# Spacing the small-matmul steps of a planned transformer kernel, with first column tiles interleaved

## The chip, the cores and the metric

The kernel runs on one core of a Trainium2 chip. Times are device microseconds from start to end of one execution. The kernel before takes 2018.91 us, the median of three runs (2014.14 to 2020.16).

## The reference, cut to what matters

A sequence of 256 positions with 1024 features goes through two blocks of two layers, all in fp32. A layer of the first block is a gated feed-forward (2816 wide), an attention mixer, and a second gated feed-forward. A layer of the second is a mixer of three branches and a feed-forward with a short convolution.

```python
def first_block(x, ...):
    for l in range(2):
        x = x + 0.5 * swiglu(rms_norm(x, norm_ffn1[l]), ...)
        x = x + hybrid_mixer(rms_norm(x, norm_mix[l]), ...)   # NSA heads (8) and MoBA heads (8), then w_out
        x = x + 0.5 * swiglu(rms_norm(x, norm_ffn2[l]), ...)
    return rms_norm(x, norm_final)

def second_block(x, ...):
    for l in range(2):
        p = rmsnorm(x, norm1_g[l]) @ w_in[l]
        p_rw, p_ret, p_sg, gate_logits = jnp.split(p, in_cuts, axis=-1)
        branches = jnp.stack([rwkv7_branch(p_rw, ...), retention_branch(p_ret, ...), sgu_branch(p_sg, ...)], axis=2)
        proj = jnp.einsum('bsgc,gcd->bsgd', branches, w_branch[l])
        x = x + jnp.sum(sigmoid(gate_logits) * proj, axis=2) @ w_out[l]
        x = x + conv_ffn(rmsnorm(x, norm2_g[l]), ...)
    return rmsnorm(x, final_g)

# the end of rwkv7_branch: a recurrence over the positions, then a norm by head
    y = rwkv7_scan(r, decay, k, v, kk, a)
    mean = jnp.mean(y, axis=-1, keepdims=True)
    var = jnp.mean(jnp.square(y - mean), axis=-1, keepdims=True)
    y = (y - mean) * lax.rsqrt(var + RW_GN_EPS) * lnx_g + lnx_b
    y = y + jnp.sum(r * k * r_k, axis=-1, keepdims=True) * v     # the "bonus"
    return y * g
```

NSA attention adds three gated parts for each head: attention over compressed keys, over selected keys and over a window. MoBA is attention over blocks of keys. Both are softmax attention with masks.

## The kernel before, in words

Every large product is done in three matmuls. ACT rounds a weight tile of 128x1024 (`raw`) to a high part `wh`, DVE subtracts it to get the low part `wl`, and the activations have a high and a low part too (`xx`, `yTh` and `yTl`, `oTh`, `h` and `hl`). The products are wh by high, wl by high and wh by low. In the profile they are the tiles `pj` (projections), `cf` (up projections of the feed-forwards) and `acc` (products back to 1024 features). They are the main stream, written out in the order of the layers. All weights come from device memory once, by transfers that SP issues.

Everything else is a side task: a Python generator that issues a few instructions, and yields until something is ready. A planner (`Builder`, with a clock for each engine in `Meter`) orders the instructions while the program is built; on the chip each engine then runs its instructions in that fixed order and waits for semaphores. After each group of main matmuls the main stream calls `tick`, which issues weight transfers, and then runs the steps of side tasks that are ready by the planner's clock, those of the lowest rank first. Where the main stream needs a side task's result, it calls `need`. That runs side steps one after the other until the result is planned, and no main matmul comes between.

The attention mixer (`mixer1`) projects queries, keys, values and gates, and runs the attention as side steps under the later projections and under the output product (`acc` from `oT`). `compressed` is the branch over compressed keys: scores `sc`, a softmax on DVE and ACT (`cs`, `cm`, `ce`), transposes, `pv`. `attend` handles the other parts: scores `sc`, a minimum on DVE (`sm`, `mn`), exponentials on ACT (`pe`), a product on DVE with `rsum`, transposes into PSUM (`pt`), a copy by ACT (`pts`), and the product with the values (`pv`).

The mixer of the second block (`mixer2`) first projects the RWKV columns (`mixed`, seven column tiles of 256, each in two halves of the depth). Side tasks then make the keys, queries and products of the recurrence. `rw_queries` lets POOL make r*k, whose sum by head is a small matmul `pb` (the bonus). `rw_chain` solves the recurrence in chunks: matmuls `pS` take `sa` and `X` in turns, and give `X` (DVE) and `sa` (ACT). At its end, for each 128 positions, `pY` is added to `Y`, and `group_norm` runs on it: a mean `gm` (DVE), squares `gsq` (ACT), their sum `gs` (DVE), `var` and `rstd` (POOL), four products or sums with `Y` (DVE), and POOL's `gbv`, which is the bonus times v plus lnx_b. `Y` is then transposed (`pt`) and split into `yTh` and `yTl`. `retention` does the like for `yret` (small matmuls `rs` and `py`) and `gating` for the spatial gate (`pm`, `su`, `sv`).

The main stream of `mixer2` goes on with the projections of retention and gating, and then, for each branch b in the order 1 (retention), 2 (gating), 0 (RWKV), with two halves of gates and two halves of the branch's projection (`proj`, PSUM ring "ps"), whose result DVE multiplies into `gate`. A branch's projection calls `need` for its `yTh`.

`load_wc` brings the five tiles of the weights that compress keys and values (`wc`), 2.6 MB, ahead of an attention mixer. It is called when the phase before that mixer begins, which in the first layer is at the start of the program.

Of the kernel before, what the change touches and what calls it, by code (L numbers as in the profile page):

```python
# [27 lines left out]
BIG = 3.0e38  # L28
# [173 lines left out]
class Task:  # L202
# [3 lines left out]
    def __init__(self, gen, rank):  # L206
        self.gen, self.rank = gen, rank
        self.ready = 0.0
        self.cond = None


ROWS = {"w0": 0, "lnx_g": 512, "lnx_b": 1024, "ln_g": 1536, "ln_b": 2048}
RWC = {"mu": (0, 14), "a0": (14, 4), "k_k": (18, 4), "k_a": (22, 4), "r_k": (26, 4)}
RET, SG, GATE = 1792, 3328, 4352
RW_GROUPS = (("wag", 1536, 256), ("k", 512, 512), ("r", 0, 512), ("v", 1024, 512))
# [2 lines left out]
LEAD = 1  # L218
FIRST = 2
PARTS, SKEW = 2, 2  # L220


class Builder:
    def __init__(self, tc, ctx, A, out):
        self.tc, self.A, self.out = tc, A, out
        self.meter = Meter()
        nc = self.nc = Engines(tc.nc, self.meter)
        self.cp = ctx.enter_context(tc.tile_pool(name="cp", bufs=1))
        self.wp = ctx.enter_context(tc.tile_pool(name="wp", bufs=NRAW))
        self.up = ctx.enter_context(tc.tile_pool(name="up", bufs=5))  # L230
        self.sp = ctx.enter_context(tc.tile_pool(name="sp", bufs=1))
        self.pp = ctx.enter_context(tc.tile_pool(name="pp", bufs=8, space=bass.MemoryType.PSUM))
        self.dp = ctx.enter_context(tc.tile_pool(name="dp", bufs=2, space=bass.MemoryType.DRAM))
        self.tasks = []
        self.plan, self.dma_next, self.high_next, self.split_next, self.take_next = [], 0, 0, 0, 0
        self.freed = self.lagged = 0
        self.raws, self.highs, self.parts = {}, {}, {}
        self.halves = [2, 2]
# [31 lines left out]
        self.tasks.sort(key=lambda x: x.rank)  # L270

    def step(self, task):
        self.meter.last = self.meter.t["PE"]
        try:
            y = next(task.gen)
        except StopIteration:
            self.tasks.remove(task)
            return
        if y is None:
            task.ready = self.meter.last + 0.1  # L280
        elif isinstance(y, float):
            task.ready = self.meter.last + y
        elif callable(y):
            task.cond = y
        else:
            task.ready = self.meter.of(y) + 0.1
# [10 lines left out]
    def tick(self, limit=3.0):  # L297
        m = self.meter
        end = m.t["PE"] + limit
        between = any(x.rank < 0 for x in self.tasks)  # L300
        if not between:
            self.fetch(self.lagged)
        while m.t["PE"] < end:
            late = m.t["DVE"] > m.t["PE"] + 5.0
            task = next((x for x in self.runnable() if x.ready <= m.t["PE"] and not (late and x.rank > 2)), None)
            if task is None:
                break
            self.step(task)
        if between:
            self.fetch(self.lagged, PACE)  # L310
        self.lagged = self.freed
# [877 lines left out]
    def mixer2_plan(self, l):  # L1189
        w_in, w_b = self.A["w_in_2"][l], self.A["w_branch_2"][l]  # L1190

        def cols(c0, n=512):
            self.proj_plan(w_in, 0, KD, c0, n)

        def branch(b):
            for hf in range(2):
                self.proj_plan(w_b[b], 0, 4, hf * 512, 512)

        for _, c0, n in RW_GROUPS:
            for c in range(c0, c0 + n, 2 * P):  # L1200
                for k0 in (0, 4):
                    self.plan.append((self.rows_of(w_in, k0 * P, 4, c, 2 * P), 4, 2 * P))
        for c0 in (RET, RET + 512, RET + 1024, SG + 512, SG):
            cols(c0)
        for b in (1, 2, 0):
            cols(GATE + b * D)
            cols(GATE + b * D + 512)
            branch(b)
        self.accum_plan(self.A["w_out_2"][l], 0, KD)

    def mixed(self, l, st, name, c0, n):


        nc = self.nc
        factor, factored = self.factor, self.factored
        done = st.setdefault("mixed", [])
        m = []

        def mix(i, ps):
            f0 = c0 // P + 2 * i  # L1220
            yield lambda: len(factored) == NT
            yield factor
            R = factor[0][:, None, :S].to_broadcast([P, 2, S])
            u, o = self.u("up"), self.pairs(name)
            uv, ov = (x.rearrange(v, e=2) for x, v in ((u, "p (e s) -> p e s"), (o.rearrange("p e t f -> p (e t f)"), "p (e s) -> p e s")))
            nc.vector.tensor_tensor(uv, ps.rearrange("p (e s) -> p e s", e=2), R, ALU.mult)
            done.append(name)
            yield
            for e in range(2):
                nc.scalar.activation(ov[:, e], uv[:, e], AF.Copy, scale=st["omu"][:, f0 + e:f0 + e + 1])  # L1230
            yield
            for e in range(2):
                nc.vector.scalar_tensor_tensor(ov[:, e, 1:], uv[:, e, :-1], st["mu"][:, f0 + e:f0 + e + 1], ov[:, e, 1:],
                                               ALU.mult, ALU.add)
            m.append(o)
            yield
            if len(m) == n // (2 * P):
                st[name] = m

        for i in range(n // (2 * P)):  # L1240
            at = st["banks"] = st.get("banks", -1) + 1
            self.need(lambda: len(done) > at - (3 if at == 6 else 4))
            ps = self.ps("pj", "pq" if at == 6 else ("ps", "pq")[at % 2])
            for k0 in (0, 4):
                self.need(lambda: min(self.ready_xT) > k0 // 4)
                wh, wl = self.take(4, 2 * P)
                xs = [[x[:, k0 + k].rearrange("p t f -> p (t f)") for x in (self.xh, self.xl)] for k in range(4)]
                for f in range(2):
                    c = slice(f * S, (f + 1) * S)
                    w = slice(f * P, (f + 1) * P)  # L1250
                    for k in range(4):
                        for j, (a, b) in enumerate(((wh, xs[k][0]), (wh, xs[k][1]), (wl, xs[k][0]))):
                            nc.tensor.matmul(ps[:, c], a[:, k, w], b, start=k0 + k + f + j == 0,
                                             stop=k0 + k == KD - 1 and j == 2, skip_group_check=True)
                        if k == 3 and f == 1:
                            self.free()
                        self.tick()
            self.begin(mix(i, ps), 0)

    def mixer2(self, l, after):  # L1260
# [6 lines left out]
        st = {}  # L1267
# [24 lines left out]
        def branch(b, hf):  # L1292
            def get(kk, t):
                self.need(lambda: (b, t) in yT)
                h, lo = yT[b, t]
                return h[:, kk], lo[:, kk]

            def evac(t, ps):
                g = gates[b, hf][t]
                nc.vector.tensor_tensor(g, ps, g, ALU.mult)  # L1300
                if (hf, t) in G:
                    nc.gpsimd.tensor_tensor(G[hf, t], G[hf, t], g, ALU.add)
                else:
                    G[hf, t] = g

            self.proj(get, 4, 512, evac)

        GT = {}

# [306 lines left out]
    def rw_queries(self, l, st):  # L1616
# [9 lines left out]
        for q in range(2):  # L1626
            nc.gpsimd.tensor_tensor(r[q], r[q], k[q], ALU.mult)
        yield r
        pb = self.ps("pb")
        for t in range(NT):  # L1630
            for j in range(4):
# [49 lines left out]
    def rw_chain(self, l, st, done):  # L1681
# [57 lines left out]
            return sa  # L1739

        S0 = None
        for t in range(NT):
            if t:
                pX = self.ps("pX")
# [28 lines left out]
                    mm(pY2[:, j * P:(j + 1) * P], kr[j // 2][:, j % 2, t, 1], S0[:, j], start=True, stop=True)  # L1773
                tt(Y[t], pY2, Y[t], ALU.add)
            yield
            self.begin(self.group_norm(lnx, Y[t], v[t], st["bonus"][t], st["g"][t], lambda y, t=t: done(t, y)), 3)

    def group_norm(self, lnx, y, v, bonus, g, done):
        nc = self.nc
        tt = nc.vector.tensor_tensor  # L1780
        heads, wide = self.heads, self.wide
# [2 lines left out]
        nc.vector.tensor_scalar(m, m, 1.0 / 64, None, ALU.mult)  # L1784
        tt(heads(y), heads(y), wide(m), ALU.subtract)
        yield
        sq, bv = self.u("gsq"), self.u("gbv")
        nc.scalar.activation(sq, y, AF.Square)
        nc.gpsimd.tensor_tensor(heads(bv), heads(v), wide(bonus), ALU.mult)
        nc.gpsimd.tensor_tensor(bv, bv, lnx[1], ALU.add)  # L1790
        yield [sq]
        s2 = self.small("gs", 8)
        nc.vector.tensor_reduce(s2, heads(sq), AX.X, ALU.add)
# [21 lines left out]
def emit(tc, A, out, upto=None):  # L1815
    with ExitStack() as ctx:
# [39 lines left out]
        def enter(i, t):  # L1856
            if t == 0 and any(ph[0] != "norm" for ph in phases[i:]):
                b.new_xT()
            b.begin(before(i, t), -1 - i)

        gain(0)
        b.fetch(-NSPLIT, most=FIRST)
        b.load_x(1)
# [3 lines left out]
        for i, (kind, l, gi, w) in enumerate(phases):  # L1867
            gain(i + 1)
            if i + 1 < len(phases) and phases[i + 1][0] == "mix1" or kind == "mix1" and i == 0:
                b.wc = []  # L1870
                b.load_wc(phases[i + 1][1] if kind != "mix1" else l, 0, 5)
            b.rows_next = i + 1 == len(phases) or (phases[i + 1][0] == "norm" and True)
            after = lambda t: enter(i + 1, t)
            if kind == "ffn":
# [24 lines left out]
```

## Time and profile before

| what | value |
| --- | --- |
| median of three runs | 2018.91 us |
| profiled execution | 2018.39 us, span 2016.6 us, mean clock 0.994 |
| TensorE (PE) busy | 1973.9 us, 98% |
| DVE busy | 1395.5 us, 69% |
| ACT busy | 1084.6 us, 54% |
| POOL busy | 153.2 us, 8% |
| DMA | 343.85 MB, mean 171 GB/s |

All compute instructions have the line of one helper (L191), so a group is known by its tiles, as `pt<-ident,Y`: output, then inputs. PE is TensorE's matmuls, PEld its weight loads. In a row of the timeline the first column is the start, the second the duration of the group, x the number of instructions in it; in brackets stand the idle time of that engine ahead of it and what ended it. In a row of the windows, each engine has its busy time and its instructions, then come the granted clock of TensorE (1.00 is 2.4 GHz, 0.50 is 1.2 GHz), the share of DMA and its rate. The layers follow each other: the attention mixers lie at 199 to 338 us and 709.5 to 849 us, the mixers of the second block at 1034.5 to 1329.5 us and 1528.5 to 1814 us. The rest is feed-forward.

### The profile page before, as it was taken

The numbers are of one execution on the slowest core, as the hardware profiler recorded it, in microseconds if no ns is written. First come the engines' busy times: TensorE is split into PE (matmuls) and PEld (weight loads), VectorE is DVE, ScalarE is ACT, GpSimd is POOL, SyncE is SP. The second block draws the span as 40 slices with busy tenths as digits, with TensorE's granted clock in tenths as the row PEclk, the third lists the DMA queues.
The fourth block names the chain that finished last, engine by engine and source line by source line (L and its number), as shares of the span: only waits on it lengthen the run. The fifth ranks groups of instructions, "written<-read, shape, count | busy, mean of one in ns | idle before, by whom it ended". The sixth has DMA issues, their size and how long they took to land. (4 is left out here: it accounts for less than half of the span.)

```text
span 2016.6 us, 31964 instructions
## 1 busy us (share of the span) xinstructions
PE 1973.9 (98%) x12396; PEld 1694.9 (84%) x12396; DVE 1395.5 (69%) x2201; ACT 1084.6 (54%) x1753; POOL 153.2 (8%) x176
## 2 busy tenths in 40 slices
PE   8999999999999999999999999999999999999998
PEld 6898877898889887788888767899988777889997
DVE  5764676765666467577567957579956796668983
ACT  5653666654555367565447443456646544446652
POOL 0000100000000010000021031210001004110000
PEclk9999999999999999999999999999999899999999
DMA  8664733666765563366664344556565443565663
GB/s 283 221 191 153 216 95 115 190 197 186 228 196 177 182 199 104 99 207 180 195 192 137 108 139 134 185 175 188 182 195 169 128 147 111 171 192 182 186 190 95
DMA packets 246726, 343.85 MB, mean 171 GB/s; under 512 B 22064, under 2 KB 182192, under 8 KB 246448
## 3 DMA queue, kind: packets, MB, share of 16 engines
q1 hardware_dynamic: 244224, 340.20, 54.7%
q8 instruction: 97, 1.59, 0.3%
q10 hardware_dynamic: 2352, 1.63, 0.3%
q14 instruction: 53, 0.43, 0.1%
HBM read 339.68 MB, written 2.10 MB: 169 GB/s over the span
## 5 line engine op out<-in xcount | busy, mean ns | idle before, releaser
L191 DVE TENSOR_TENSOR wl<-raw,wh 128x1024 fp32r<-128x1024 f32 (+1 forms) x614 | 750.8, 1235 | 262.8 <-ACT wh L191 262.0
L191 ACT CAST wh<-raw 128x1024 fp32r<-128x1024 f32 (+1 forms) x614 | 638.0, 1047 | 531.8 <-PE cf L191 176.8
L191 PE MATMUL cf<-xx,wh 128*128 128x256 f32 (+1 forms) x3072 | 544.0, 325 | 4.7 <-ACT wh L191 4.0
L191 PEld LDWEIGHTS cf<-xx,wh 128*128 128x128 f32 x3072 | 446.5, 191 | 43.0 <-ACT wh L191 4.8
L191 PE MATMUL pj<-wh,xx 128*128 128x512 f32 (+1 forms) x1088 | 364.9, 398 | 2.4 <-ACT rg L191 0.9
L191 PE MATMUL cf<-xx,wl 128*128 128x256 f32 x2112 | 295.7, 283 | 1.3 <-DVE wl L191 1.3
L191 PEld LDWEIGHTS cf<-xx,wl 128*128 128x128 f32 x2112 | 280.7, 191 | 12.8 <-DVE wl L191 1.7
L191 PEld LDWEIGHTS pj<-wh,xx 128*128 128x128 f32 x1088 | 204.3, 189 | 54.0 <-issue 8.4
L191 PE MATMUL pj<-wl,xx 128*128 128x512 f32 (+1 forms) x544 | 210.7, 387 | 0.0
L191 PE MATMUL acc<-wh,h 128*128 128x512 f32 x528 | 207.0, 392 | 0.0
L191 PE MATMUL acc<-wh,hl 128*128 128x512 f32 x528 | 205.6, 389 | 0.0
L191 PE MATMUL acc<-wl,h 128*128 128x512 f32 x528 | 205.5, 389 | 0.0
L191 PEld LDWEIGHTS pj<-wl,xx 128*128 128x128 f32 x544 | 103.0, 189 | 17.1 <-DVE wl L191 1.0
L191 PEld LDWEIGHTS acc<-wh,hl 128*128 128x128 f32 x528 | 99.1, 188 | 20.9
L191 PEld LDWEIGHTS acc<-wl,h 128*128 128x128 f32 x528 | 99.2, 188 | 19.9
L191 PEld LDWEIGHTS acc<-wh,h 128*128 128x128 f32 x528 | 99.2, 188 | 19.9
L191 POOL TENSOR_SCALAR xv<-ss 128x1 f32<-128x1 f32 x24 | 15.8, 660 | 1120.7 <-ACT junk L191 1120.6
L191 DVE TENSOR_TENSOR up<-cf,up 128x256 f32<-128x256 f32 x144 | 54.1, 418 | 67.1 <-ACT up L191 67.1
L191 PE MATMUL pj<-xx,wh 128*128 128x256 f32 x448 | 85.5, 290 | 3.4 <-DVE xx L191 2.0
L191 ACT CAST xx<-xg 128x512 fp32r<-128x512 f32 x40 | 24.9, 621 | 105.0 <-DVE xg L191 104.7
L191 DVE SCALAR_TENSOR_TENSOR cs<-up,conv,cs 128x255 f32<-128x255 f32 (+1 forms) x176 | 77.2, 480 | 0.4
L191 PEld LDWEIGHTS pj<-xx,wh 128*128 128x128 f32 x448 | 70.0, 191 | 8.5 <-issue 3.3
(314 smaller groups left out, 2231.3 us busy)
## 6 DMA issues: line engine op xcount, KB each, us to landing
raw<-w_in SPq DMA_DIRECT2D x156, 512.0 KB, 4.3
raw<-w_ffn_gate SPq DMA_DIRECT2D x88, 512.0 KB, 4.6
raw<-w_ffn_up SPq DMA_DIRECT2D x88, 512.0 KB, 4.8
raw<-w_ffn_down SPq DMA_DIRECT2D x88, 512.0 KB, 4.3
raw<-ffn_w_up SPq DMA_DIRECT2D x88, 512.0 KB, 4.5
raw<-ffn_w_down SPq DMA_DIRECT2D x44, 512.0 KB, 4.3
raw<-w_out SPq DMA_DIRECT2D x32, 512.0 KB, 3.7
raw<-w_branch SPq DMA_DIRECT2D x24, 512.0 KB, 3.9
```

The lines of the kernel that those rows point to most:

```text
L191: return f(*args, **kw)
```

## The change

1. `APART`: the planner notes for each place in a side task's code whether the step from there used TensorE (`kinds`), and when the last such step ended on the planner's clock (`burst`). In `tick`, a task of rank 0 or more, whose next step is known to use TensorE, is not run within 4 us after the last such step. `need` has no such rule.
2. `mixed`: the first halves of the first two column tiles come one after the other, then their second halves. The plan of the weight tiles follows.
3. `rw_queries` yields for 1.2 us on the planner's clock between POOL's r*k and the `pb` matmuls.
4. `gbv` moves out of `group_norm` into `offsets`, which is called for both halves of the positions when the last part of `rw_chain` begins.
5. The second half of the projection of the last branch uses the PSUM ring "pq" in place of "ps".
6. Where a feed-forward stands before an attention mixer, `load_wc` is called tile by tile by a side task (`later`), after 16, 20, 24, 28 and 32 weight tiles of that phase.

```diff
+APART = 4.0
 def step(self, task):
+        at, t0 = task.at(), m.t["PE"]
...
+        if m.t["PE"] > t0:
+            self.burst = m.t["PE"]
+            self.kinds[at] = True
+        else:
+            self.kinds.setdefault(at, False)
 def tick(self, limit=3.0):
+        apart = m.t["PE"] < self.burst + APART
...
-            task = next((x for x in self.runnable() if x.ready <= m.t["PE"] and not (late and x.rank > 2)), None)
+            task = next((x for x in self.runnable() if x.ready <= m.t["PE"] and not (late and x.rank > 2)
+                         and not (apart and x.rank >= 0 and self.kinds.get(x.at(), False))), None)
 def mixed(self, l, st, name, c0, n):
+        for i in range(n // (2 * P)):
+            early = st.pop("early", None)
+            if early is not None:
+                ps = early
+            else:
+                ps = bank()
+                products(ps, 0)
+            if st["banks"] == 0:
+                st["early"] = bank()
+                products(st["early"], 0)
+            products(ps, 4)
 def mixer2(self, l, after):
-            self.proj(get, 4, 512, evac)
+            self.proj(get, 4, 512, evac, "pq" if b == 0 and hf else "ps")
 def rw_queries(self, l, st):
         yield r
+        yield 1.2
         pb = self.ps("pb")
 def rw_chain(self, l, st, done):
+        bvs = [self.offsets(lnx, v[t], st["bonus"][t]) for t in range(NT)]
...
-            self.begin(self.group_norm(lnx, Y[t], v[t], st["bonus"][t], st["g"][t], lambda y, t=t: done(t, y)), 3)
+            self.begin(self.group_norm(lnx, Y[t], bvs[t], st["g"][t], lambda y, t=t: done(t, y)), 3)
 def emit(tc, A, out, upto=None):
+        def later(l, base):
+            for n in range(5):
+                yield lambda: b.take_next >= base + 16 + 4 * n
+                b.load_wc(l, n, n + 1)
...
-                b.load_wc(phases[i + 1][1] if kind != "mix1" else l, 0, 5)
+                if kind == "mix1":
+                    b.load_wc(l, 0, 5)
+                else:
+                    b.begin(later(phases[i + 1][1], b.take_next), 0)
```

The order of TensorE's instructions in the first attention mixer, in the NSA part (`sc` scores, `pt` transposes of `pe`, `pv` products with values, `pj` projections of the main stream). Before:

```order
L191 MATMUL pt<-ident,pe 128x128 x4
L191 MATMUL pj_2613<-wh,xx 128x512
L191 MATMUL pj_2613<-wl,xx 128x512
L191 MATMUL pj_2613<-wh,xx 128x512
L191 MATMUL pj_2614<-wh,xx 128x512
L191 MATMUL pj_2614<-wl,xx 128x512
L191 MATMUL pj_2614<-wh,xx 128x512 x2
L191 MATMUL pj_2614<-wl,xx 128x512
L191 MATMUL pj_2614<-wh,xx 128x512
L191 MATMUL pv<-pts,kv_1942 64x128 x2
L191 MATMUL pv<-pts,kv_2122 64x128 x2
```

The same place in the changed kernel, TensorE again:

```order
L191 MATMUL pt<-ident,pe 128x128 x4
L191 MATMUL pv<-pts,kv_1942 64x128 x2
L191 MATMUL pv<-pts,kv_2097 64x128 x2
L191 MATMUL sc<-kh,qst 128x512
L191 MATMUL sc<-kl,qst 128x512
L191 MATMUL sc<-kh,qst 128x512
L191 MATMUL sc<-kl,qst 128x512
L191 MATMUL pt<-ident,pe 128x128 x4
```

Nine projection matmuls stood between the transposes and the `pv` that needs ACT's copy of them; now none does. In the first layer no projection matmul comes after the transposes of `ce`, in the second only three come after the last transposes of the queries.

TensorE's order at the end of the recurrence of the second layer of the second block. Before (`pj_16788` is a gate's projection; the transposes of this `Y` come 60 main matmuls after the last `pY`):

```order
L191 MATMUL pY<-sa,mrb 64x64 x16
L191 MATMUL pY_16950<-S_16648,kr 128x128 x4
L191 MATMUL pj_16788<-wh,xx 128x512
L191 MATMUL pj_16788<-wl,xx 128x512
L191 MATMUL pj_16788<-wh,xx 128x512 x2
```

The same place after (`pj_17421` and `pj_17422` are the projection of the last branch, which needs `yTh`):

```order
L191 MATMUL pj_17421<-wh,yTl 128x512
L191 MATMUL pS<-sa,Lo 32x64 x4
L191 MATMUL pS<-X,dbd 32x64 x4
L191 MATMUL pY<-sa,mrb 64x64 x16
L191 MATMUL pY_17465<-S_16968,kr 128x128 x4
L191 MATMUL pt<-ident,Y 128x128 x4
L191 MATMUL pj_17422<-wh,yTh 128x512
```

The end of the recurrence moved into the last branch. Its transposes now follow the last `pY` at once; in the first layer three main matmuls stand between. The `pS` steps ahead of it stand 21 main matmuls apart.

TensorE's order in the second layer where the first branch (`pj_16636`, `pj_16637`) asks for the result of retention, `yret`, after:

```order
L191 MATMUL pj_16636<-wh,yTl 128x512
L191 MATMUL pX<-vt,lm 64x64 x2
L191 MATMUL pY<-vt,lm 64x64 x2
L191 MATMUL pX<-vt,lm 64x64 x2
L191 MATMUL pY<-vt,lm 64x64 x2
L191 MATMUL py<-rv,rsc 128x128
...
L191 MATMUL pt<-ident,yret 128x128 x4
L191 MATMUL pt<-ident,su 128x128 x4
L191 MATMUL pj_16637<-wh,yTh 128x512
```

Here side steps alone stand between two main matmuls; before, this branch found all of `yret` planned.

## Rows read from the trace of the kernel before

**Rows 1.** The page's head.

```profile
span 2016.6 us, 31964 instructions
PE 1973.9 (98%) x12396; PEld 1694.9 (84%) x12396; DVE 1395.5 (69%) x2201; ACT 1084.6 (54%) x1753; POOL 153.2 (8%) x176
```

**Rows 2.** Windows of the four mixers: busy time by engine, then clock and DMA.

```profile
199.00:338.00 139.00, 135.47 (x867) 107.41 (x866) 94.88 (x273) 90.74 (x213) 7.16 (x11) 1.00 0.43 133
709.50:849.00 139.50, 135.97 (x871) 107.93 (x870) 95.11 (x275) 91.28 (x214) 8.02 (x12) 1.00 0.44 136
1034.50:1329.50 295.00, 282.63 (x1860) 229.63 (x1858) 210.30 (x318) 149.99 (x235) 56.68 (x55) 0.98 0.48 150
1528.50:1814.00 285.50, 279.37 (x1838) 226.91 (x1836) 206.61 (x311) 145.33 (x228) 48.09 (x43) 0.98 0.50 155
```

**Rows 3.** Windows of an attention tail and of the stretches at half clock.

```profile
286.00:302.00 16.00, 13.86 (x119) 10.34 (x116) 10.53 (x26) 10.35 (x28) 0.00 (x0) 1.00 0.15 45
1103.84:1110.64 6.80, 6.71 (x26) 5.98 (x26) 5.22 (x15) 3.66 (x6) 0.04 (x1) 0.50 0.65 232
1240.40:1243.70 3.30, 3.30 (x9) 2.55 (x8) 2.05 (x3) 0.58 (x1) 0.00 (x0) 0.50 0.80 253
1592.00:1602.10 10.10, 10.10 (x42) 8.22 (x41) 4.92 (x14) 2.91 (x5) 1.36 (x1) 0.50 0.37 123
```

**Rows 4.** TensorE's waits: us in total, times, longest.

```profile
PE pj L191 <- DVE gate L191: 3.3, 2, 2.8
PE pb L191 <- POOL r L191: 2.0, 2, 1.4
PE pt L191 <- DVE v L191: 1.6, 1, 1.6
```

**Rows 5.** Timeline of the start, TensorE.

```profile
27.30 2.14 PE L191 MATMUL cf<-xx,wh 128*128 128x512 f32 x8 [1.31 <-ACT wh L191]
33.52 0.74 PE L191 MATMUL cf<-xx,wl 128*128 128x256 f32 x4 [1.30 <-DVE wl L191]
```

**Rows 6.** Timeline of a main run between small matmuls: its first, and the next small.

```profile
1111.69 0.50 PE L191 MATMUL pj<-wh,xx 128*128 128x512 f32 x1
1113.96 0.34 PE L191 MATMUL pX<-vt,lm 128*64 128x64 f32 x4
```

**Rows 7.** Timeline of the first NSA attention, TensorE.

```profile
282.64 0.66 PE L191 MATMUL pv<-pts,kv 128*64 128x128 f32 x8
284.62 0.47 PE L191 MATMUL pj<-wh,xx 128*128 128x512 f32 x1
288.83 1.57 PE L191 MATMUL pv<-pts,kv 128*64 128x128 f32 x16 [0.68 <-ACT pts L191]
291.76 0.43 PE L191 MATMUL pv<-pts,kv 128*64 128x128 f32 x2 [0.34 <-ACT pts L191]
```

**Rows 8.** Timeline of the compressed branch's softmax, first and last step, DVE.

```profile
255.33 0.29 DVE L191 SCALAR_TENSOR_TENSOR cs<-sc,cst 128x128 f32<-128x128 f32 x1 [0.36 <-PE sc L191]
260.75 0.29 DVE L191 TENSOR_TENSOR ce<-ce,cm 128x128 f32<-128x128 f32 x1
```

**Rows 9.** Timeline of the end of the first recurrence: DVE, TensorE, ACT.

```profile
1226.64 0.69 DVE L191 TENSOR_TENSOR Y<-pY,Y 128x512 f32<-128x512 f32 x1 [0.39 <-PE pY L191]
1234.29 0.69 DVE L191 TENSOR_TENSOR Y<-Y,rstd 128x512 f32<-128x512 f32 x1 [1.84 <-POOL rstd L191]
1238.21 1.28 DVE L191 TENSOR_TENSOR gate<-pj,gate 128x512 f32<-128x512 f32 x2
1238.95 0.50 PE L191 MATMUL pj<-wh,yTh 128*128 128x512 f32 x1 [2.80 <-DVE gate L191]
1240.39 0.59 ACT L191 CAST yTh<-pt 128x512 fp32r<-128x512 f32 x1 [3.11 <-PE pt L191]
```

**Rows 10.** Timeline of the end of retention, TensorE.

```profile
1182.12 0.48 PE L191 MATMUL py<-R,qs 64*128 64x128 f32 x2
1186.08 0.60 PE L191 MATMUL pt<-ident,yret 128*128 128x128 f32 x4
```

More of the change, by code (lines that the diff above doesn't have):

```diff
@@ L209, in __init__, with at @@
         self.cond = None
+    def at(self):
+        r, g = [], self.gen
+        while g is not None and getattr(g, "gi_frame", None) is not None:
+            r.append((g.gi_code.co_name, g.gi_frame.f_lineno))
+            g = g.gi_yieldfrom
+        return tuple(r)
 ROWS = {"w0": 0, "lnx_g": 512, "lnx_b": 1024, "ln_g": 1536, "ln_b": 2048}
@@ L234, in __init__ @@
         self.tasks = []
+        self.kinds, self.burst = {}, -BIG
         self.plan, self.dma_next, self.high_next, self.split_next, self.take_next = [], 0, 0, 0, 0
@@ L272, in step @@
     def step(self, task):
-        self.meter.last = self.meter.t["PE"]
+        m = self.meter
+        at, t0 = task.at(), m.t["PE"]
+        m.last = t0
         try:
@@ L277, in step @@
             self.tasks.remove(task)
-            return
+            y = 0.0
+        if m.t["PE"] > t0:
[3 more added lines that the diff above has]
+            self.kinds.setdefault(at, False)
         if y is None:
@@ L1197, in branch @@
                 self.proj_plan(w_b[b], 0, 4, hf * 512, 512)
[L1199 to L1202, printed above, removed]
+        tiles = [c for _, c0, n in RW_GROUPS for c in range(c0, c0 + n, 2 * P)]
+        for c, k0 in [(c, k0) for k0 in (0, 4) for c in tiles[:2]] + [(c, k0) for c in tiles[2:] for k0 in (0, 4)]:
+            self.plan.append((self.rows_of(w_in, k0 * P, 4, c, 2 * P), 4, 2 * P))
         for c0 in (RET, RET + 512, RET + 1024, SG + 512, SG):
@@ L1238, in mix, with products @@
                 st[name] = m
-        for i in range(n // (2 * P)):
+        def products(ps, k0):
+            self.need(lambda: min(self.ready_xT) > k0 // 4)
+            wh, wl = self.take(4, 2 * P)
+            xs = [[x[:, k0 + k].rearrange("p t f -> p (t f)") for x in (self.xh, self.xl)] for k in range(4)]
+            for f in range(2):
+                c = slice(f * S, (f + 1) * S)
+                w = slice(f * P, (f + 1) * P)
+                for k in range(4):
+                    for j, (a, b) in enumerate(((wh, xs[k][0]), (wh, xs[k][1]), (wl, xs[k][0]))):
+                        nc.tensor.matmul(ps[:, c], a[:, k, w], b, start=k0 + k + f + j == 0,
+                                         stop=k0 + k == KD - 1 and j == 2, skip_group_check=True)
+                    if k == 3 and f == 1:
+                        self.free()
+                    self.tick()
@@ L1241, in mixed, with bank @@
+        def bank():
             at = st["banks"] = st.get("banks", -1) + 1
             self.need(lambda: len(done) > at - (3 if at == 6 else 4))
[L1243 to L1257, printed above, removed]
+            return self.ps("pj", "pq" if at == 6 else ("ps", "pq")[at % 2])
@@ L1775, in rw_chain, with offsets, group_norm @@
             yield
-            self.begin(self.group_norm(lnx, Y[t], v[t], st["bonus"][t], st["g"][t], lambda y, t=t: done(t, y)), 3)
-    def group_norm(self, lnx, y, v, bonus, g, done):
+            self.begin(self.group_norm(lnx, Y[t], bvs[t], st["g"][t], lambda y, t=t: done(t, y)), 3)
+    def offsets(self, lnx, v, bonus):
+        nc = self.nc
+        bv = self.u("gbv")
+        nc.gpsimd.tensor_tensor(self.heads(bv), self.heads(v), self.wide(bonus), ALU.mult)
+        nc.gpsimd.tensor_tensor(bv, bv, lnx[1], ALU.add)
+        return bv
+    def group_norm(self, lnx, y, bv, g, done):
         nc = self.nc
@@ L1786, in group_norm @@
         yield
-        sq, bv = self.u("gsq"), self.u("gbv")
+        sq = self.u("gsq")
         nc.scalar.activation(sq, y, AF.Square)
-        nc.gpsimd.tensor_tensor(heads(bv), heads(v), wide(bonus), ALU.mult)
-        nc.gpsimd.tensor_tensor(bv, bv, lnx[1], ALU.add)
         yield [sq]
```

## The prediction

> **What bounds the kernel now.** I read the page's head first, then the stages as windows, then TensorE's waits, then the timeline around each wait. TensorE is busy 1973.9 of 2016.6 us [rows 1], so there are only some 43 us that a change of order can win, and everything that uncovers TensorE is lost at full price. By stage [rows 2], the two attention mixers have 139.00 − 135.47 = 3.5 us and 139.50 − 135.97 = 3.5 us without a matmul. The two RWKV mixers have 295.00 − 282.63 = 12.4 us and 285.50 − 279.37 = 6.1 us; their mean clock is 0.98, the attention mixers' 1.00. The clock loss is in three stretches of 6.80, 3.30 and 10.10 us at 0.50, that is 1.2 instead of 2.4 GHz [rows 3], each soon after a wait: for POOL's r (two waits, 2.0 together), for DVE's gate (two waits, up to 2.8) and for DVE's v (1.6) [rows 4]. Half of 20.2 us is 10.1 us lost. The reader is to see that TensorE is the bound, and that what is left lies in the mixers' small steps: idle time, the clock after it, and the change of shapes.
>
> The sum is made against the profiled execution, 2018.4 us. The median of the runs is 2018.9, half a us more, and I add that at the end.
>
> **The change part by part.**
>
> Later wc loads. At the start five wc transfers stand on SP ahead of the second weight tiles. TensorE waits 1.31 us for ACT's wh and 1.30 us for DVE's wl [rows 5]. Without those transfers both can go: −2.6 us (bounds 0 and −2.6). The same five issues come later, among weight loads of stages where TensorE waits for no transfer; I cost them at nothing, with up to +1.3 us if a weight tile comes late once, as there.
>
> Column tiles two by two, and r*k with a pause ahead of the pb matmuls. No matmul is added. They work only on idle time in the RWKV stages, and are priced with it below.
>
> Fewer returns to the main stream. A run of nine 128x512 matmuls between small ones takes from 1111.69 to 1113.96, 2.27 us [rows 6], where nine at the steady 0.227 us would take 2.04: 0.23 us for one small-to-large turn. The order has 184 main runs in the mixers where it had 224. I take 0.2 us for each of the 40: −8.0 us (bounds 0 and −9.2).
>
> The distance in the attention mixers. The distance holds a side step back while main matmuls remain, so the main stream runs out earlier, and what is left runs in `need` with nothing between. The pieces of order show it: four attend steps that had 3 to 9 projection matmuls between transposes and pv now have none. ACT must copy the transposes out before pv can start. Where before has no cover either, pv waits 0.68 and 0.34 us for it (the last two of rows 7). In the four, ACT has four exponentials and two copies in a row with nothing between them for TensorE, so I take 0.85 us each, above both waits: 3.4 us. With 0.6 us for the compressed branch's transposes the first layer loses 4.0 us. In the second layer the compressed branch's DVE chain, 255.33 to 261.04 or 5.7 us [rows 8], loses its cover too; some 1.3 us of scores lie beside it, so 4.4 us more: 8.4. In MoBA all scores now come in one go, and the first transposes wait for a whole chain of minimum, exponential, sum and product; the nearest row is half of the DVE chain of rows 8, 2.9 us, and I take 3.2 us in the first layer and 4.4 us in the second, where two more scores lose their cover. Together 4.0 + 8.4 + 3.2 + 4.4 = +20.0 us (bounds: 8.8 with 0.34 us for each of 26 steps, 26 with 1 us for each).
>
> The distance in the RWKV mixers. It spreads the chain's pS and X steps to one every 21 matmuls, so their waits of up to 1.7 us find DVE and ACT done. Of the 12.4 and 6.1 us idle I let 1.6 and 1.7 stay, since the way into the stage is unchanged: −10.8 and −4.4 us (bounds 0 and −12.4, 0 and −6.1). With the waits go the three slow stretches, −5.05 us in each layer.
>
> But the chain now ends in the last branch. Before, 60 matmuls stood between the last pY and its transposes, now three in the first layer and none in the second. The path is Y, mean, square, variance, POOL's power, four products with Y, transposes, cast: from 1226.64 to ACT's cast at 1240.39, 13.75 us [rows 9]. Of this 0.6 us was another tile's DVE work ahead of the mean, 0.5 a gate on ACT ahead of the square, and some 2.6 the transposes standing behind the stalled gate matmul: about 10.1 us remain with nothing else on the engines. In the first layer 0.9 us of TensorE work lies beside it, +9.2. In the second less does, and two pS steps stand bare ahead of it: +10.6. The bonus's POOL work is out of this path, but it was not on it: DVE waits 1.84 us for rstd there, not for gbv. The other ring for the last branch lets its first bank be taken without waiting for the gate products; that wait is the 2.80 us of rows 9, in the idle already taken off.
>
> Retention is late in the same way, since branch 1 now asks for it. From the last py at 1182.12 to the transposes at 1186.08 is 3.96 us [rows 10]; less 0.4 of py itself and with up to 0.7 of small steps beside it, +2.8. In the second layer py and rs stand in the uncovered piece too: +3.5. Each layer then has a wait of some 10 us, and the three waits of before, all shorter, were each followed by a stretch at 1.2 GHz; the mean of these is 6.7 us, 3.4 us lost. So +3.4 in each layer. That gives first layer −10.8 − 5.05 + 9.2 + 2.8 + 3.4 = −0.5, second −4.4 − 5.05 + 10.6 + 3.5 + 3.4 = +8.0.
>
> The clock in the attention tails. From 286 to 302 us TensorE is busy 13.86 of 16.00 us with waits in between, and the clock stays at 1.00 [rows 3]. The new bare pieces are longer and idler than that; I take one slow stretch of the mean size, +3.4 us (bounds 0 and the rival below). The Trainium skill says otherwise (TensorE: Matmul & The Clock Gate, "A second HAM failure mode: psum-queue depth-cycling"): frequent small pauses between groups of matmuls are enough to make the clock swing between its two levels. The row at 286 does not agree, the bare pieces here have more pauses than it; by that rule the second rival is what happens.
>
> Sum: −2.6 − 8.0 + 20.0 − 0.5 + 8.0 + 3.4 = +20.3. 2018.4 + 20.3 = 2038.7, with the half us of the median 2039.
>
> **The rivals.**
>
> A, the clock falls through all the bare attention steps. For: they are alternations of wait and small matmuls, and three other waits brought 1.2 GHz. Against: the 16 us at 286. A step's TensorE work (pv, scores, transposes) takes from 282.64 to 284.62, 1.98 us [rows 7]. At half the clock it takes 3.96, where my 1.98 + 0.85 makes 2.83: 1.1 us more in each of the 22 bare NSA steps (10 and 12), +24, less the 3.4 counted: 2060.
>
> B, the distance doesn't do what it says: it is measured on the planner's clock, and a step is known to be a matmul step only after it has run once, so the waits of the RWKV mixers move but stay. Half of the 15.2 us of idle and the 10.1 us of slow clock come back: 2039 + 7.6 + 10.1 = 2057. For: the 1.6 us for v comes from no dense burst. Against: the order, where the spread is plainly there.
>
> C, faster. The place is the last branch: if what DVE, ACT and POOL no longer do in between makes the chain after pY short enough to hide, it costs nothing, and neither does retention. Then 2039 − 9.2 − 10.6 − 2.8 − 3.5 − 6.8 = 2006. It decides from about 45 matmuls of cover after pY. Against: the order has at most 3 there, and the chain's POOL and DVE steps need 10 us by themselves.
>
> D, about even: bare attention steps wait 0.34 us as in the last row of rows 7 (−11), and the chain at the end is half as long (−10): 2018.
>
> **How the numbers follow.** What a measurement can tell of this kernel is about 0.3%, 6 us. Forecast 2039 at 0.62, with its own range 2027 to 2052; A 0.11, B 0.10, C 0.10, D 0.07. The range 2012 to 2059 leaves out C and half of A. Faster by over 0.3% is C, 0.10; within it D, 0.07; slower the forecast, A and B, 0.83.
>
> **What would show it.** In the profile after: TensorE idle in the attention stages of 10 to 20 us in place of 3.5 each, the pv waits for ACT pts about 20 in number; a single wait of 5 to 10 us for Y's transposes near the end of each RWKV mixer, with the pS waits gone; the waits at 27.30 and 33.52 gone; no 0.50 stretch after pb. Wrong would be: attention stages as long as before (the bare steps cost nothing), the last wait under 4 us, or the clock at 0.50 for more than 20 us in the attention mixers.

## The result and the profile after

The changed kernel takes 2063.16 us, the median of four runs (2062.09 to 2065.1), where the kernel before takes 2018.97. The ratio is 1.0226, with an interval of 1.021 to 1.0241: 2.3% slower, 44 us. The forecast was 2039 us with a range to 2059.

The page's head and the clock line of the changed kernel, in the profiled execution:

```profile
span 2060.3 us, 31982 instructions
PE 1981.8 (96%) x12396; PEld 1705.0 (83%) x12396; DVE 1388.1 (67%) x2201; ACT 1086.2 (53%) x1753; POOL 155.2 (8%) x176
PEclk9999999999999999999999999999999999989999
```

Each compute engine has the same number of instructions as before [rows 1]. TensorE is busy 7.9 us more, though it computes the same, and the span is 43.7 us longer. To see where, each mixer is cut at the same two instructions in both kernels: from its first `pj` matmul to the first `cf` matmul of the feed-forward behind it. These are the windows of the kernel before, then of the changed one (length, then busy time by engine as in [rows 2]):

```profile
199.90:338.00 138.10, 134.57 (x863) 106.65 (x862) 94.41 (x273) 89.84 (x212) 7.16 (x11) 1.00 0.44 134
710.80:848.70 137.90, 134.37 (x863) 106.63 (x862) 94.40 (x273) 89.83 (x212) 8.02 (x12) 1.00 0.44 138
1036.00:1337.30 301.30, 289.39 (x1892) 235.56 (x1893) 213.73 (x323) 151.00 (x237) 56.68 (x55) 0.98 0.48 148
1526.20:1821.80 295.60, 289.47 (x1893) 235.60 (x1893) 213.57 (x321) 149.33 (x233) 48.09 (x43) 0.98 0.50 153
```

```profile
196.70:338.70 142.00, 135.41 (x864) 108.11 (x863) 94.72 (x273) 90.41 (x212) 7.29 (x11) 1.00 0.42 130
711.50:861.40 149.90, 137.71 (x864) 111.05 (x863) 94.93 (x273) 90.71 (x212) 8.05 (x12) 0.97 0.41 127
1048.60:1363.50 314.90, 292.30 (x1892) 237.47 (x1893) 210.76 (x323) 150.31 (x237) 57.44 (x55) 0.96 0.47 142
1552.50:1865.50 313.00, 290.56 (x1893) 237.60 (x1892) 208.11 (x321) 149.04 (x233) 48.77 (x43) 0.96 0.48 145
```

The attention mixers grew by 3.9 and 12.0 us, the RWKV mixers by 13.6 and 17.4 us, and the first mixer begins 3.2 us earlier (196.70 in place of 199.90). Length minus busy time is TensorE's idle time: 6.6, 12.2, 22.6 and 22.4 us, where it was 3.5, 3.5, 11.9 and 6.1. What TensorE waited for, over the whole changed kernel:

```profile
PE pt L191 <- DVE Y L191: 17.0, 2, 8.8
PE pv L191 <- ACT pts L191: 6.7, 21, 1.0
PE pt L191 <- DVE ce L191: 5.3, 2, 3.0
PE pb L191 <- ACT Kh L191: 5.1, 1, 5.1
...
PE pt L191 <- DVE yret L191: 3.6, 1, 3.6
PE pb L191 <- POOL r L191: 3.2, 2, 2.6
```

Against [rows 4], the waits for gate and v have gone or shrunk, but those for r and Kh ahead of `pb` are larger, and the two waits for the last `Y` are new. Behind the longer waits stand the slow stretches. Some of their windows:

```profile
786.93:797.17 10.24, 5.83 (x25) 5.35 (x26) 6.40 (x35) 5.64 (x28) 0.00 (x0) 0.50 0.00 0
1131.68:1141.92 10.24, 8.88 (x46) 7.20 (x47) 3.94 (x13) 1.71 (x4) 0.00 (x0) 0.50 0.28 85
1319.41:1329.65 10.24, 4.54 (x12) 3.45 (x13) 4.59 (x6) 1.03 (x2) 1.85 (x2) 0.50 0.08 11
1817.76:1831.41 13.65, 6.07 (x16) 4.63 (x17) 5.73 (x8) 2.26 (x3) 1.85 (x2) 0.50 0.13 38
```

I count a slow stretch as half of TensorE's busy time in it (the second number), not half of its length, since part of it lies in the wait. With three shorter ones that makes an estimate of 20.2 us lost, where it was 10.2.

### The profile page after: what moved, and what is told of

It is laid out like the page before. It is cut to its first block, busy times and chain, and to the rows that moved or that the text cites. A ratio compares the mean times of both kernels' runs of the same rounds, so it can differ in the third digit from the quotient of the medians.

```text
span 2060.3 us, 31982 instructions
## 1 busy us (share of the span) xinstructions
PE 1981.8 (96%) x12396; PEld 1705.0 (83%) x12396; DVE 1388.1 (67%) x2201; ACT 1086.2 (53%) x1753; POOL 155.2 (8%) x176
## 4 chain that ended last, share of the span: by engine, by line
PE 89%; DVE 3%; ACT 3%; POOL 1%; DMA 1%; issue 1%; SPq 0%; DVEq 0%; POOLq 0%; ACTq 0%
PE cf L191 36%; PE acc L191 22%; PE pj L191 22%; PE pt L191 3%; PE pv L191 1%; PE pS L191 1%; DVE wl L191 1%; PE sc L191 1%; ACT pe L191 1%; ACT pts L191 1%; DVE Y L191 1%; PE pM L191 0%; PE pY L191 0%; DMA sysd<-Ld 0%; PE py L191 0%
## 5 line engine op out<-in xcount | busy, mean ns | idle before, releaser
L191 PE MATMUL pj<-wh,xx 128*128 128x512 f32 (+1 forms) x1088 | 356.1, 396 | 2.7 <-ACT sv L191 1.7
```

The costliest lines, as they stand in the source:

```text
L191: return f(*args, **kw)
```

## The experiments

Theory 1 was that the distance alone makes the loss: it pushes the side steps out of the cover of the main stream. Theory 2 was that the other parts of the change make the loss in the RWKV mixers. All runs were compared with the kernel before on the same chip. Of the rows of a trace only those that the text reads are shown; others lie between them.

**Which part.** In `no_distance`:

```diff
-APART = 4.0
+APART = -BIG
```

> The changed kernel with the distance set to nothing, all other parts kept. Theory 1 (the distance alone makes the loss, by pushing side steps out of the cover of the main stream): the start keeps its 3.2 us, attention and RWKV mixers go back to about the idle time of before, 2006 to 2017 us. Theory 2 (the tiles taken two by two, the pause ahead of pb and the sums moved ahead make the loss of the RWKV mixers): attention goes back, but the RWKV mixers keep their 31 us, 2040 to 2050 us.

Measured 2008.36 us, ratio 0.9959 (0.9942 to 0.9975), a little faster than before. The mixers take 138.3, 137.9, 294.9 and 295.7 us. Theory 2 falls. `distance_alone` puts part 1 of the change into the kernel before and nothing else.

> The kernel before with the distance of 4 us alone. Theory 1: start as before, everything else as in the changed kernel, 2060 to 2072 us. Theory 2: only the attention mixers' 16 us, about 2035 us, with the RWKV mixers as before.

Measured 2073.66 us, ratio 1.029 (1.026 to 1.0321). Theory 1 holds. By the ratios, the distance costs 54 us with the other parts and 58 us without them, and the other parts give back 13 and 8 us. `two_us` has `APART = 2.0`.

> The changed kernel with a distance of 2 us in place of 4. If the loss grows with how far the steps are pushed (theory 1), it is well under half of that at 4 us, since most steps of a chain then still end under the main stream: 2010 to 2035 us, the waits for the last Y below 4 us. If any distance at all breaks the order in which tasks take turns, it stays above 2050 us.

Measured 2019.42 us in one run. The loss is far less than half. TensorE idles 1.9 and 5.8 us less in the attention mixers and 13.4 and 9.3 us less in the RWKV mixers than with 4 us, and the waits for the last `Y` are 0.7 us or less.

**The end of the recurrence.** `until_gates` drops the distance in `mixer2` from the first gate's projection on; each later phase begins with it again (that line and the starting value are left out here):

```diff
-        apart = m.t["PE"] < self.burst + APART
+        apart = self.spaced and m.t["PE"] < self.burst + APART
...
         gates, G = {}, {}
+        self.spaced = False
```

> The changed kernel with the distance dropped in the RWKV mixers from the first gate projection on, so that the end of the recurrence is again issued close together, some 50 main matmuls ahead of its transposes. If the late chain makes the loss at the end of these mixers (theory 1), the waits for the last Y (8.1 and 8.8 us) and most of the slow clock behind them go, some 12 us per layer: 2035 to 2042 us, while the waits of the front part (pb, 5.1 and 3.2 us) stay. Rival: the bursts that come back bring their own waits and slow stretches back, and the time stays above 2050 us.

Measured 2030.36 us, ratio 1.0074 (1.0057 to 1.0092). This is below what I expected: the RWKV mixers are 12.6 and 19.5 us shorter, where I had some 12 for each. TensorE around the last `Y` of the first one:

```profile
1264.99 1.16 PE L191 MATMUL pY<-S,kr 128*128 128x128 f32 x8
1278.94 0.60 PE L191 MATMUL pt<-ident,Y 128*128 128x128 f32 x4
```

The same chain of DVE, ACT and POOL, 14 us here from the start of `pY`, is now no wait at all, since main matmuls stand between.

**The waits at pb.** In the changed kernel, SP, POOL, ACT and TensorE around the wait of 5.09 us:

```profile
1123.89 1.10 SPq L191 DMA_DIRECT2D Lc<-sysd  x2
1128.67 0.15 POOL L191 MEMSET Lc<- 128x32 f32 x1 [30.13 <-DMA Lc<-sysd]
1128.78 2.51 POOL L191 TENSOR_TENSOR r<-r,k 128x512 f32<-128x512 f32 x2
1128.86 2.04 ACT L191 COPY Lt<-Lc 128x512 f32<-128x512 f32 x2 [4.74 <-POOL Lc L191]
1132.33 0.57 ACT L191 COPY Kh<-pt 128x512 f32<-128x512 f32 x1
1133.05 3.12 PE L191 MATMUL pb<-rwo,r 128*128 128x2 f32 x14 [5.09 <-ACT Kh L191]
```

A transfer through device memory (`sysd` to `Lc`) is issued at 1123.89. POOL's small memset waits for it, and r*k stands behind the memset in POOL's queue. ACT's copies `Lt` wait for the memset, and `Kh` stands behind them. `pb` needs r, which is done at 1131.29, and a tile of the ring of four PSUM tiles that `Kh` reads from; `Kh` is done at 1132.90, and the trace names it as what ended the wait. `chain_later` moves the memset to where the recurrence starts, and that 5 us later:

```diff
-        nc.gpsimd.memset(Lc.rearrange("p s t -> p (s t)")[:, 0::33], 1.0)
...
+        yield 5.0
+        nc.gpsimd.memset(st["Lc"].rearrange("p s t -> p (s t)")[:, 0::33], 1.0)
         kr, off, T = (st[n] for n in ("kr", "off", "T"))
```

> The changed kernel with the start of the recurrence (POOL's memset on Lc, ACT's copies Lt) 5 us later on the planner's clock, so that POOL's r*k and ACT's Kh do not stand behind an instruction that waits for a transfer through device memory. If TensorE's waits at pb (5.1 us in the first RWKV mixer, 3.2 us in the second) come from that in-order queue, they fall below 1 us and the mixers get 5 to 10 us shorter with the clock behind them. If they come from POOL's own r*k being late, they stay.

Measured 2042.25 us in one run; the RWKV mixers are 10.8 and 9.0 us shorter, and no wait at `pb` is left above 0.4 us. POOL in this run:

```profile
1120.83 2.14 POOL L191 TENSOR_TENSOR r<-r,k 128x512 f32<-128x512 f32 x1 [22.32 <-DVE kr L191]
1125.41 1.71 POOL L191 TENSOR_TENSOR r<-r,k 128x512 f32<-128x512 f32 x1 [2.43 <-DVE k L191]
1128.37 0.16 POOL L191 MEMSET Lc<- 128x32 f32 x1 [1.25 <-DMA Lc<-sysd]
```

r*k now runs ahead of the memset, so the waits at `pb` came from the order in the queues of POOL and ACT. `both_away` has both edits.

> The changed kernel with the start of the recurrence 5 us later and the distance dropped from the first gate projection on; the attention mixers keep the distance. If the waits at pb and the late end are separate, the losses add: 2063 less 33 and 21 us less what retention then waits, 2008 to 2016 us, which is front_only plus the 16 us of the attention mixers. If one hides the other, it stays above 2022 us.

Measured 2014.8 us in one run, 48 us less than the changed kernel, where the two edits alone take away 33 and 21 us. So the two losses are separate in the main, and add up but for some 5 us.

**The clock.** `fill` puts 36 matmuls on data at hand into each of the two waits for the last `Y`:

```diff
-            self.begin(self.group_norm(lnx, Y[t], bvs[t], st["g"][t], lambda y, t=t: done(t, y)), 3)
+            self.begin(self.group_norm(lnx, Y[t], bvs[t], st["g"][t], lambda y, t=t: done(t, y), t == 1), 3)
...
         yield 2.0
+        if fill:
+            ps, x = self.ps("fill"), self.xx
+            for i in range(36):
+                raw = nc.tensor.engine
+                raw.matmul(ps, x[:, 0, 0, 0], x[:, 0].rearrange("p e t f -> p (e t f)"), start=True, stop=True)
         yield from done(y)
```

> The changed kernel with 36 more 128x512 matmuls, whose result nobody reads, in front of the transposes of the last Y in both RWKV mixers, where TensorE waits 8.1 and 8.8 us. If the slow clock after these waits is paid for by the wait itself, the clock stays at 1.00 there and the kernel gets 4 to 6 us shorter although it does more (5.2 and 6.7 us of matmuls ran at half clock behind the waits). If the slow stretches have another cause, the time stays within 1 us or grows by what the 36 matmuls reach beyond the wait, and 0.50 is still seen.

Measured 2058.21 us, ratio 1.0207 (1.0189 to 1.0225). By the ratios alone this is not clear of the changed kernel, but its trace tells it. The windows after the two waits:

```profile
1319.80:1330.00 10.20, 9.53 (x42) 7.16 (x41) 5.67 (x8) 1.98 (x3) 1.71 (x2) 1.00 0.18 51
1818.00:1831.00 13.00, 11.69 (x54) 8.95 (x53) 8.48 (x10) 2.72 (x4) 4.27 (x3) 1.00 0.17 45
```

The clock is 1.00 where it was 0.50, and the mixers are 2.8 and 2.7 us shorter, although they do more (in the first, some 0.8 us of this is another slow stretch, from 1207.17, that was shorter in this run). So these two slow stretches come from the waits.

**The other parts.** `ring_back` undoes the other PSUM ring, `sums_back` puts POOL's `gbv` back into `group_norm`, both without the distance.

```diff
-            self.proj(get, 4, 512, evac, "pq" if b == 0 and hf else "ps")
+            self.proj(get, 4, 512, evac)
```

```diff
-        bvs = [self.offsets(lnx, v[t], st["bonus"][t]) for t in range(NT)]
...
         nc.scalar.activation(sq, y, AF.Square)
+        bv = self.offsets(lnx, *bv)
```

> The kernel without the distance, with the last branch back on its old PSUM ring. If the other ring is what took the 2.8 us wait for DVE's gate and the slow 3.4 us behind it out of the first RWKV mixer, this mixer gets 3 to 5 us longer again, 2011 to 2014 us. If the sums moved ahead did it, nothing changes, 2007 to 2010 us.

> The kernel without the distance, with POOL's gbv sums back in the norm by head. If POOL's memset of sa standing behind these sums made the 1.75 us wait of the first RWKV mixer before (and the gate's 2.8 us came from the chain being late by it), both come back: this mixer 3 to 7 us longer, 2011 to 2015 us. If the two column tiles by turns made that gain, nothing changes, 2006 to 2010 us.

Measured 2007.18 and 1998.57 us, one run each. The ring does nothing that this run shows. The sums moved ahead cost some 10 us, and neither of my two answers had that. POOL, ACT, DVE and TensorE of the second RWKV mixer of `no_distance`:

```profile
1655.42 1.04 POOL L191 TENSOR_TENSOR gbv<-vt,bs 128x512 f32<-128x512 f32 x1
1661.19 0.52 POOL L191 MEMSET sa<- 128x512 f32 x1
1661.75 0.36 ACT L191 COPY sa<-pS 32x256 f32<-32x256 f32 x1 [6.07 <-POOL sa L191]
1662.02 0.57 ACT L191 CAST yTh<-pt 128x512 fp32r<-128x512 f32 x1
1662.62 0.69 DVE L191 TENSOR_TENSOR yTl<-pt,yTh 128x512 fp32r<-128x512 f32 x1 [4.88 <-ACT yTh L191]
1663.23 0.75 DVE L191 TENSOR_TENSOR rsc<-rs,cst 128x256 f32<-128x256 f32 x2
1663.79 0.77 PE L191 MATMUL py<-rv,rsc 128*128 128x128 f32 x2 [2.85 <-DVE rsc L191]
```

Four sums hold POOL from 1655.42 to 1661.19 ahead of the memset of `sa`. ACT's copy waits 6.07 us, DVE stands behind ACT, and TensorE behind DVE. `distance_sums_back` asks whether they do so in the changed kernel.

> The changed kernel with POOL's sums back in the norm by head. With steps 21 matmuls apart, the sums ahead of the memset of sa should find room, and the last Y does not wait for gbv: no change, 2060 to 2066 us. If they hold ACT's sa and yTh up there as well, the RWKV mixers get 5 us or more shorter, below 2058 us; if their place in the norm makes the last Y later, over 2066 us.

Measured 2062.82 us in one run: no. The sums do hold ACT in the changed kernel: it waits 11.4 us for the memset of `sa` there, and 2.4 us in this run. But the time is the same, so with the steps 21 matmuls apart these waits of ACT cost TensorE nothing that shows.

**Versions to beat both.** `nd_chain_later` joins `no_distance` and `chain_later`. `low_ranks` has a distance of 2 us, in the second block alone and for ranks 0 to 2.

```diff
-                         and not (apart and x.rank >= 0 and self.kinds.get(x.at(), False))), None)
+                         and not (apart and 0 <= x.rank <= 2 and self.kinds.get(x.at(), False))), None)
```

> The kernel without the distance, with the start of the recurrence 5 us later as well. Its wait at pb of 2.05 us in the first RWKV mixer and the slow stretch of 6.8 us behind it should go: 2002 to 2006 us, against 2008.4 without it. Rival: the later start makes the end of the chain late and takes it back, 2008 us or more.

> The changed kernel with a distance of 2 us, in the second block only, and only for tasks of rank 0 to 2, so that retention, gating and the norm by head are not held back. Attention as before; the RWKV mixers without the yret waits of the 2 us run (5.4 and 3.4 us) and with the 3.5 us of slow-clock loss that it has in place of 13 us without distance: 1998 to 2006 us. Rival: the waits are moved once more, 2008 us or more.

Measured 2007.84 us, ratio 0.9957 (0.9944 to 0.997), and 2025.04 us, ratio 1.0042 (1.0023 to 1.006): two misses. In the first the wait at `pb` went, but waits of 3.1 and 4.3 us for `yret` came. In the second retention had 5.5 and 8.6 us of them. Two edits that each take a wait away can move it on. `front_only` has the distance of 4 us in the RWKV mixers alone, until the gates, and the recurrence 5 us later; `front_two_us` the same with 2 us; `front_sums_back` is `front_only` with the sums back:

```diff
+            b.spaced = kind == "mix2"
...
         gates, G = {}, {}
+        self.spaced = False
```

> The parts of the experiments that shortened the changed kernel, put together: the distance of 4 us in the RWKV mixers only, dropped from the first gate projection on, and the start of the recurrence 5 us later. If the three losses add up (attention 16 us, the waits at pb some 20, the end of the recurrence some 32, of which a part is gain beyond the kernel before), the RWKV mixers come to some 291 and 285 us and the kernel to 1992 to 2000 us. Rival: with the front part pushed back, retention is asked for too early, its waits take the gain back, and it is no better than without distance, 2006 us or more.

> The same with a distance of 2 us. If a shorter distance leaves more time for retention ahead of the first branch, its waits are smaller than with 4 us: 1992 to 2002 us. Rival: the waits do not depend on the distance, and it equals the run with 4 us within 3 us.

> The best so far (distance in the front part of the RWKV mixers only, recurrence 5 us later, 1998.8 us) with POOL's sums back in the norm by head. Without the distance they cost 9 us. If it is the same queue of POOL that made the 3.2 us wait for sa in the second RWKV mixer, 1990 to 1996 us. If there is no more to win since nearly all idle time there is gone, 1996 to 2000 us.

Measured 1998.84 us, ratio 0.9913 (0.9896 to 0.993); 2008.17 us, ratio 0.9961 (0.9947 to 0.9976); and 1991.55 us, ratio 0.9871 (0.9854 to 0.9887). The last is 26 us faster than the kernel before. Its RWKV mixers:

```profile
1033.50:1319.00 285.50, 282.98 (x1893) 231.50 (x1894) 212.98 (x323) 150.46 (x237) 56.42 (x55) 1.00 0.50 157
1507.90:1795.20 287.30, 285.58 (x1893) 234.23 (x1892) 211.74 (x321) 149.78 (x233) 52.47 (x43) 0.99 0.50 157
```

2.5 and 1.7 us of idle time are left, and two slow stretches of 3.4 us in the second. Where there is main work to come, a distance of 4 us pays here: `nd_chain_later` differs from `front_only` in the distance alone and is 9 us slower. With 2 us the second RWKV mixer gave the gain back (300.2 us, where `front_only` has 291.0). POOL, DVE, TensorE and ACT there, in `front_two_us`:

```profile
1651.65 1.27 POOL L191 TENSOR_TENSOR ws<-ws,cst 128x512 f32<-128x512 f32 x1 [26.66 <-DMA ws<-ws]
1655.25 1.12 DVE L191 SCALAR_TENSOR_TENSOR yret<-py,rstd,rg 128x128 f32<-128x128 f32 x4 [9.65 <-POOL rstd L191]
1655.74 1.16 PE L191 MATMUL pt<-ident,yret 128*128 128x128 f32 x4 [4.53 <-DVE yret L191]
1661.67 0.36 ACT L191 COPY sa<-pS 32x256 f32<-32x256 f32 x1 [14.77 <-POOL sa L191]
```

It is POOL's queue once more: its step on `ws` waits for a transfer, retention's `rstd` stands behind it, and the four sums then stand ahead of the memset of `sa`. Two slow stretches there cost an estimated 7.7 us. This is read from the trace; no run tested it.

## Why the prediction was wrong

The direction was right, and so was the mechanism of what the distance adds: work made late, run bare in `need`. Wrong was what it was to take away in the RWKV mixers, and the size came out at half. Term by term, in us, measured from the windows above (clock: half of the busy time in stretches at 0.50; fewer returns: the change of what is left of busy time in the four mixers; the sums are of unrounded terms on the right, and on the left as the prediction has it):

| term | predicted | measured |
| --- | --- | --- |
| start | −2.6 | −3.2 |
| attention, idle | +20.0 | +11.7 |
| attention, clock | +3.4 | +2.9 |
| RWKV, idle | +1.2 and +9.7 | +10.7 and +16.3 |
| RWKV, clock | −1.65 and −1.65 | +4.3 and +2.9 |
| fewer returns to the main stream | −8.0 | −1.7 |
| sum | +20.3 | +43.7 |

**The step that failed** is "Of the 12.4 and 6.1 us idle I let 1.6 and 1.7 stay". The late ends came as sized. The waits for `Y` are 8.13 and 8.84 us and those for `yTh` behind them 0.68 and 0.67, against 9.2 and 10.6. The chain of the first, on DVE, TensorE and ACT:

```profile
1315.64 0.69 DVE L191 TENSOR_TENSOR Y<-pY,Y 128x512 f32<-128x512 f32 x1 [0.39 <-PE pY L191]
1324.44 1.08 PE L191 MATMUL pt<-ident,Y 128*128 128x128 f32 x4 [8.13 <-DVE Y L191]
1325.56 0.59 ACT L191 CAST yTh<-pt 128x512 fp32r<-128x512 f32 x1 [6.91 <-PE pt L191]
```

Retention's waits, with those of the bare steps beside them, are some 6.0 and 4.2 us, against 2.8 and 3.5. Without them 7.8 and 8.8 us of idle time remain in the two mixers, not 1.6 and 1.7. The largest part of that is the wait at `pb`: 5.09 us in the first, 2.58 and 0.63 us in the second, where a wait of 2.06 us for DVE's gate is new too. I wrote off the waits of before as a cost of bursts. [Rows 4] named POOL's r, and I did not follow r back to what stood ahead of it on POOL, a memset that waits for a transfer. In the kernel before:

```profile
1101.25 0.15 POOL L191 MEMSET Lc<- 128x32 f32 x1 [23.07 <-DMA Lc<-sysd]
1101.36 2.51 POOL L191 TENSOR_TENSOR r<-r,k 128x512 f32<-128x512 f32 x2
```

A distance does not shorten that queue: before, in the changed kernel and in `two_us` the memset comes 4.6 to 4.8 us after SP issues the transfer. What differs is the work that TensorE has between that issue and `pb`, in the first layer 4.9 us before, 4.1 us in the changed kernel, and 8.8 us in `two_us`, which has no wait at `pb`. `chain_later` takes the queue away, and shows what it cost.

**The clock** followed from this: I counted the three old slow stretches as gone, with one new one per layer, and there are six in the two mixers. The one forecast for the attention mixers is there. My own sign, no stretch at 0.50 after `pb`, failed: one of 10.24 us lies there. `fill` shows that the waits for the last `Y` make the two behind them, and in `chain_later` the two behind `pb` are gone. The other two, from 1206.77 and 1776.80, begin in a wait of 3.60 us for `yret` and behind that of 2.06 us for the gate; no run took these waits away alone.

**Fewer returns.** One run of nine matmuls [rows 6] was carried to 40 turns. By the traces, the four mixers have 186 main runs before, 149 in the changed kernel and 189 in `no_distance`. Taking idle time and clock off, its four mixers are 2.4 us shorter in sum, not longer. So joining 40 main runs saved nothing that shows. That small matmuls of two shapes then border on each other and pay the same is a guess that was not measured.

**Attention** was a little over half as dear as sized. TensorE in the bare NSA steps of the first layer:

```profile
278.22 0.60 PE L191 MATMUL pt<-ident,pe 128*128 128x128 f32 x4
279.06 0.93 PE L191 MATMUL pv<-pts,kv 128*64 128x128 f32 x8 [0.24 <-ACT pts L191]
278.63 0.65 ACT L191 COPY pts<-pt 128x256 f32<-128x256 f32 x2 [0.56 <-PE pt L191]
```

A bare NSA step waits 0.24 to 0.33 us, the lower end of the bounds and not 0.85. ACT is not late: it waits 0.56 us for the transposes, and begins to copy the first tile, at 278.63, while the second is transposed. The waits for `ce` (2.97 and 2.36 us) came as 5.3 against 4.4, in the second layer alone.

**The rivals.** A, slow clock through all the bare steps, did not happen. From 272 to 293 us the changed kernel has nothing but such steps, from there to 300 us eight main matmuls (`acc`) among them, and the clock stays:

```profile
272.00:300.00 28.00, 24.75 (x192) 18.65 (x192) 21.00 (x92) 22.10 (x78) 0.00 (x0) 1.00 0.17 55
```

The Trainium skill (TensorE: Matmul & The Clock Gate, "A second HAM failure mode: psum-queue depth-cycling") tells of a kernel in which frequent small pauses between groups of matmuls made the clock swing. This trace does not agree for waits of 0.24 to 0.75 us. (The prediction calls the rival that would follow from this the second; it is A.) In the attention mixers the clock fell to 1.2 GHz once, at 786.93, inside the first of the two waits for `ce`:

```profile
788.99 0.45 PE L191 MATMUL pt<-ident,ce 128*128 128x128 f32 x1 [2.97 <-DVE ce L191]
791.79 0.44 PE L191 MATMUL pt<-ident,ce 128*128 128x128 f32 x1 [2.36 <-DVE ce L191]
```

B, waits moved and not removed, came nearest, at 2057. That is luck in part: with my own term for attention put right it would have been low, and its reason, the planner's clock, is not what the runs showed. I gave it 0.10. C names what `until_gates` and `front_only` are: the cover it asked for is there, and so is the gain. D's small waits in attention came true, its shorter chain did not: 1315.64 to 1325.56, 9.92 us, is the bare chain, against 10.1 from [rows 9].

## What to carry to other kernels

A rule that spaces small steps out delays whatever they lead to, and its price stands at the last consumer: apply it only where enough main work is still to come, and let the end of a chain run close. Before counting a wait as gone, follow its releaser back through its own engine's queue; if an instruction there waits for a transfer, moving the consumer helps only as far as other work then stands beside that transfer. Moving work of an idle engine ahead is not free either, since what stands behind it in that queue may be what the busy engine needs.

## What was not expected of the hardware

Nine waits of 0.24 to 0.75 us in 28 us of mostly small matmuls (272 to 300 us) left TensorE at 2.4 GHz, while in a wait of 2.97 us the clock fell 0.9 us after its start (at 786.93) and stayed at 1.2 GHz for 10.24 us. In a wait of 8.1 us the clock fell before the wait ended (at 1319.41, with the next matmul at 1324.44), so what the slow stretch of 10.24 us cost behind it was, by my estimate, 2.3 us, half of 4.54, and not 5.1.
